# Tokens in another order in SBUF for each pair of feature tiles, in a gated short-convolution layer

## The chip, the core and the metric

The kernel runs on one core of a Trainium2 chip. The metric is the device time of one execution in microseconds; the profile is of one execution on that core. Engines are called as the profile calls them: PE is TensorE, with PEld for its weight loads; DVE is VectorE, ACT is ScalarE, SP the queue that issues nearly all DMAs.

## The reference

One layer, on 256 tokens of 2048 features, in float32. The normalised input is scaled and shifted by a vector that depends on the condition `c`, goes through a large projection to four times 4096 features, a causal convolution of width 3 with gates, and a projection back; then comes a gated residual and a last norm.

```python
h = rmsnorm(x, norm_g[0])
mod = silu(c) @ ada_w[0] + ada_b[0]
shift, scale, gate = split(mod, 3)
h = h * (1 + scale) + shift
b_gate, c_gate, v, g = split(h @ w_in, 4)       # w_in: 2048 x 16384
u = causal_depthwise_conv(c_gate * v, conv_w)   # width 3
y = (b_gate * u * silu(g)) @ w_out              # w_out: 4096 x 2048
out = rmsnorm(x + gate * y, final_g)
```

## The kernel before

**Products in three parts.** Every large product is taken in `float32r`, which keeps fewer bits of the mantissa. To keep float32's accuracy, each operand is split into a high part, rounded to `float32r`, and a low part, the rest. One product becomes three that are added in PSUM: weights high with tokens high, weights high with tokens low, weights low with tokens high.

**The tile of tokens.** `hT` (L272) holds the modulated input, features on the partitions: 16 feature tiles of 128 features, and for each tile a row of 512 words in each partition, the 256 tokens' high parts and behind them the 256 low parts. `hh_` and `hl_` (L273, L274) are views of the two halves. `modulate` (L293) fills it, for two feature tiles at a time: ACT writes the high part (L300), DVE computes the full value in place (L301) and writes the low part (L304).

**The first projection.** The weights are the stationary operand (128 features by 128 outputs), the tokens the moving one (128 features by 256 tokens). `product` (L440) issues one of the three matmuls for a feature tile `k`, at L444. A 128-output tile takes 16 × 3 matmuls of 256 columns, and there are 128 of them, so 6144 in all. PSUM banks hold two such outputs, and only the first matmul into a bank clears its flags (`start`); the other output's first matmul is ordered behind it by hand (L447).

The scale and shift take long to arrive: `ada_w` is read in pieces (`ada_piece`), summed over the rows on DVE, and each group of pieces makes two more feature tiles ready (`ada_done`, `modulate`). Therefore `plan` (L52) writes out by hand, from costs and due times, which part of which output is computed over which feature tiles while the rest is not yet there. `part` (L469) runs such a step (tiles `mm_s`, weights `raw_s`); sums that are not whole are kept in `acc`. That covers the first half of the projection, 16 of 32 column tiles in each quarter. The second half (loop from L573; tiles `mm_b`, weights `raw`) takes all 16 feature tiles at once, in two halves of eight (`KP`). The weights are split by ACT (`split_hi`, L314) and DVE (`split_lo`, L319).

**The gate of the residual** is computed beside this: 32 pieces of `ada_w` (`at_g`, L556) are summed on DVE (L563, L565), and four matmuls of ones (L568) add over the partitions. These instructions are given a lower priority (`later(GIVE)`), and the scheduler places them. It orders the instructions of each engine and queue ahead of time by a model of its own; only what `in_order`, `behind` and `issue_after` mark is fixed by hand.

**The second projection** (`out_mm`, L621) has the tokens as the stationary operand and 512 weight columns as the moving one, three matmuls again (L629 to L631), and ends with the gated residual and the norm.

Of the kernel before, what the change touches and what calls it, by code (L numbers as in the profile page):

```python
# [8 lines left out]
F32 = mybir.dt.float32  # L9
F32R = mybir.dt.float32r  # L10
AF = mybir.ActivationFunctionType
ALU = mybir.AluOpType
# [4 lines left out]
T = 256  # L17
KT = D // P
# [99 lines left out]
def short_conv_layer(ctx: ExitStack, tc: tile.TileContext, x, c, norm_g, ada_w, ada_b, w_in, conv_w, w_out, final_g, out):  # L118
    nc = tc.nc
# [16 lines left out]
    def slot(shape, name, dtype=F32):  # L136
        return slots.tile(shape, dtype, tag="slot", name=name)
# [4 lines left out]
    after = mybir.DependencyInfo(mybir.DependencyClass.NoSync, mybir.DependencyReason.DATA)  # L142
# [104 lines left out]
    bias = vec[:, KT : 3 * KT].rearrange("p (s k) -> p s k", s=2)  # L247
# [6 lines left out]
    for t in range(TT):  # L254
        for dh in range(2):
# [3 lines left out]
            else:  # L259
                nc.vector.scalar_tensor_tensor(  # L260
                    out=junk[:, t], in0=xt[t][dh], scalar=1.0, in1=xt[t][dh], op0=ALU.mult, op1=ALU.mult,
# [8 lines left out]


    hT = hpool.tile([P, KT, 2 * T], F32R, tag="big", name="hT")  # L272
    hh_ = hT[:, :, 0:T]  # L273
    hl_ = hT[:, :, T : 2 * T]  # L274
    xs = [slot([P, CT, T], f"xs{j}") for j in range(KT // CT)]

    def turn_x(j):
# [13 lines left out]
    mod = const.tile([P, 2, KT], F32, tag="mod", name="mod")  # L291

    def modulate(k0, nk, sums):  # L293

        ks = slice(k0, k0 + nk)
        sums = sums.rearrange("p (s k) -> p s k", s=2)
        nc.vector.tensor_tensor(out=mod[:, :, ks], in0=sums, in1=bias[:, :, ks], op=ALU.add)
        for k in range(k0, k0 + nk):
            hf = xs[k // CT][:, k % CT, :]
            nc.scalar.activation(hh_[:, k], hf, AF.Identity, bias=mod[:, 0, k : k + 1], scale=mod[:, 1, k : k + 1])  # L300
            nc.vector.tensor_scalar(  # L301
                out=hf, in0=hf, scalar1=mod[:, 1, k : k + 1], scalar2=mod[:, 0, k : k + 1], op0=ALU.mult, op1=ALU.add
            )
            nc.vector.tensor_tensor(out=hl_[:, k], in0=hf, in1=hh_[:, k].bitcast(F32), op=ALU.subtract)  # L304

    def hi_tile():
        return wpool.tile([P, SLOT], F32R, tag="hi", name="hi", bufs=3)
# [26 lines left out]
    def split(raw, n, lo_tag="lo"):  # L334

        return split_lo(raw, n, split_hi(raw, n), lo_tag)
# [38 lines left out]
    pieces0 = [split(raw0[:, 0 : CT * P], CT * P)]  # L375
    hi0 = [split_hi(raw0[:, k * CT * P : (k + 1) * CT * P], CT * P) for k in range(1, NK0)]
    modulate(0, NK0, sums0.rearrange("p (o f) -> p o f", o=2 * NK0)[:, :, 0])
    tp_3 = turn_x(3)
    pinned.close()
# [49 lines left out]
    def ada_done(k0, nk, gv):  # L429

        tp = psum.tile([P, 4, P], F32, tag="sm", name="tp_g", bufs=2)
        gs = const.tile([P, 4], F32, tag="gs", name="gs", bufs=2)
        for o in range(2 * nk):
            nc.tensor.transpose(tp[:, o, :], gv[:, o // nk, (o % nk) * P : (o % nk + 1) * P], ident)  # L434
        nc.vector.reduce_sum(gs[:, 0 : 2 * nk], tp[:, 0 : 2 * nk, :], axis=mybir.AxisListType.X)
        modulate(k0, nk, gs[:, 0 : 2 * nk])

    opener = [None]

    def product(dst, hi, lo, k, i, begins, left, ends):  # L440

        w, h = ((hi, hh_), (hi, hl_), (lo, hh_))[i]

        mm = last_mm[0] = nc.tensor.matmul(dst, w, h[:, k], start=begins and left, stop=ends, skip_group_check=True)  # L444
        if begins and left:
            opener[0] = mm
        elif begins:  # L447
            tc.add_manual_dep(mm.ins, opener[0].ins.name, after, reason="the bank's flags are cleared first")

    def chunk_products(bank, hi, lo, o0, k, k0, k1, seed=False, late=False):  # L450


        begins = k == k0 and not seed
        terms = [(m, i) for i in (0, 2, 1) for m in range(CT)] if late else [(m, i) for m in range(CT) for i in range(3)]
        for m, i in terms:
            o = slice(o0 + m * P, o0 + (m + 1) * P)
            product(bank[:, m, :], hi[:, o], lo[:, o], k, i, begins and i == 0, m % 2 == 0, k == k1 - 1 and (m, i) == terms[-1])

    last_mm = [None]
# [80 lines left out]
    def gate(dc):  # L540
        return gates[dc // 2][:, dc % 2, :]
# [31 lines left out]
    for ct in range(NS, NCT, 2):  # L573
        for q in QUARTERS:
            bank = psum.tile([P, CT, T], F32, tag="mm", name="mm_b")[:, 0:2]
            col = q * E + ct * P
            for kp in range(0, KT, KP):
                raw = raw_tile("raw")
                nc.sync.dma_start(
                    raw.rearrange("p (k f) -> p k f", k=KP),  # L580
                    w_in[0, kp * P : (kp + KP) * P, col : col + 2 * P].rearrange("(k p) f -> p k f", p=P),
                )
                hi, lo = split(raw, SLOT)
                for m in range(2):
                    for i in range(KP):
                        k = kp + i
                        o = slice((i * 2 + m) * P, (i * 2 + m + 1) * P)
                        for j in range(3):
                            product(bank[:, m, :], hi[:, o], lo[:, o], k, j, k == 0 and j == 0, m == 0, k == KT - 1 and j == 2)
                n_piece += 1  # L590
                if n_piece % 2 == 0:
                    gate_piece()
# [58 lines left out]
    for dc in range(4):  # L651
        dcs = slice(dc * 512, (dc + 1) * 512)

        both = [psum.tile([P, TT, 512], F32, tag="mm", name="mm_o") for _ in range(1 + (dc == 3))]
# [7 lines left out]
        for ep in range(n_ep):  # L662

            first = dc == 0 and ep == 0
# [5 lines left out]
            if dc == 3:  # L670
# [3 lines left out]
                    out=raw3, in0=raw3, in1=gate(dc).unsqueeze(1).to_broadcast([P, EP, 512]), op=ALU.mult  # L674
                )
            hi, lo = split(raw, SLOT, "raw")
# [55 lines left out]
```

## Time and profile before

| | |
|---|---|
| Median of the two runs | 913.5 us (913.44 to 913.55) |
| Span of the profiled execution | 911.9 us |
| Mean granted clock of TensorE | 0.997 |
| PE, PEld, DVE, ACT busy | 98%, 94%, 68%, 51% |
| Before the first product of L444 | 25.3 us |
| First projection (25 to 729 us), L444 | 6144 matmuls, DMA 195 to 356 GB/s by stage |
| Second projection (from 729 us), L629 to L631 | 768 matmuls of 512 columns |

The profiled execution has no time of its own beside its span; the median of the runs is 1.6 us longer than the span, which leaves out what lies around the first and the last instruction. In the profile, a matmul's duration is longer than the distance to the next one, since matmuls follow each other in a pipeline and their ends are modelled: the mean of 276 ns of a group is not what one more matmul costs. That is read from the distance between starts in the timeline. A group's row gives line, engine, operation, tiles, shapes and number, then busy time and the mean of one, then the idle time before them and what ended it.

### The profile page before, as it was taken

What the parts mean: (1) busy time and instruction counts of PE and PEld (TensorE: products, weight loads), DVE (VectorE), ACT (ScalarE), POOL (GpSimd) and SP (SyncE); (2) the same over time, 40 slices, a digit from 0 to 9 for tenths busy, and PEclk for the clock granted to TensorE, in tenths of its full rate; (3) what the DMA queues carried; (4) which work ended last, traced back from release to release, by engine and by line L of the source; (5) the groups of instructions that cost most, each with busy time, mean ns of one, the idle gap of its engine ahead of it and who ended that gap; (6) DMA issues with size and microseconds to landing.
All of it is one profiled execution on the core that took longest, in us unless ns stands there. A gap on an engine that the chain in (4) does not pass through costs nothing.

```text
span 911.9 us, 16239 instructions
## 1 busy us (share of the span) xinstructions
PE 895.7 (98%) x7047; PEld 858.5 (94%) x7047; DVE 616.2 (68%) x593; ACT 464.6 (51%) x413; POOL 0.7 (0%) x6
## 2 busy tenths in 40 slices
PE   6999999999999999999999999999999999999996
PEld 4999999999999999999999999999999988888885
DVE  4889999989888899765545555545554544555882
ACT  6768856665558756743334433444333333443333
POOL 0000000000000000000000000000000000000000
PEclk9999999999999999999999999999999999999998
DMA  9999999999998698676656665566656486655542
GB/s 309 367 371 353 365 325 351 356 369 352 338 328 275 197 359 301 201 246 197 186 188 197 200 201 186 187 195 200 200 188 188 140 331 231 203 201 186 185 139 92
DMA packets 163752, 227.65 MB, mean 250 GB/s; under 512 B 5680, under 2 KB 104160, under 8 KB 163296
## 3 DMA queue, kind: packets, MB, share of 16 engines
q1 hardware_dynamic: 163552, 226.56, 74.8%
q8 instruction: 55, 0.90, 0.4%
q14 instruction: 17, 0.14, 0.0%
q10 hardware_dynamic: 128, 0.04, 0.0%
HBM read 224.49 MB, written 2.10 MB: 248 GB/s over the span
## 4 chain that ended last, share of the span: by engine, by line
PE 94%; DMA 3%; ACT 1%; SPq 1%; DVE 0%; issue 0%; ACTq 0%
PE mm_b L444 38%; PE mm_s L444 36%; PE mm_o L631 6%; PE mm_o L629 6%; PE mm_o L630 6%; DMA raw_s<-in_sc_w_in_dram 2%; DMA at<-in_ada_w_dram 1%; SPq L210 1%; DMA x<-in_x_dram 1%; ACT hi L314 0%; PE ps_gate L568 0%; PE tp_g L434 0%; ACT acc L465 0%; DVE lo L319 0%; ACT hT L300 0%; SPq L413 0%
## 5 line engine op out<-in xcount | busy, mean ns | idle before, releaser
L444 PE MATMUL mm_s<-hT,hi 128*128 128x256 f32 x2048 | 350.5, 277 | 0.2
L444 PE MATMUL mm_b<-hT,hi 128*128 128x256 f32 x2048 | 348.8, 276 | 0.0
L444 PEld LDWEIGHTS mm_s<-hT,hi 128*128 128x128 f32 x2048 | 308.7, 188 | 1.1 <-ACT hT L300 0.4
L444 PEld LDWEIGHTS mm_b<-hT,hi 128*128 128x128 f32 x2048 | 308.7, 188 | 0.2 <-issue 0.2
L444 PE MATMUL mm_b<-hT,lo 128*128 128x256 f32 x1024 | 282.6, 276 | 0.0
L444 PE MATMUL mm_s<-hT,lo 128*128 128x256 f32 x1024 | 282.2, 277 | 0.2 <-DVE lo L319 0.2
L319 DVE TENSOR_TENSOR lo<-raw,hi 128x2048 fp32r<-128x2048 f32 (+1 forms) x66 | 148.0, 2244 | 136.8 <-ACT hi L314 136.8
L314 ACT CAST hi<-raw 128x2048 fp32r<-128x2048 f32 (+1 forms) x66 | 123.7, 1874 | 200.2 <-PE mm_b L444 156.1
L444 PEld LDWEIGHTS mm_b<-hT,lo 128*128 128x128 f32 x1024 | 192.2, 188 | 0.2 <-issue 0.2
L444 PEld LDWEIGHTS mm_s<-hT,lo 128*128 128x128 f32 x1024 | 191.7, 188 | 0.7 <-DVE lo L319 0.6
L319 DVE TENSOR_TENSOR lo<-raw_s,hi 128x2048 fp32r<-128x2048 f32 (+1 forms) x80 | 147.6, 1850 | 25.6 <-ACT hi L314 24.6
L314 ACT CAST hi<-raw_s 128x2048 fp32r<-128x2048 f32 (+1 forms) x80 | 124.2, 1559 | 72.0 <-PE mm_s L444 59.2
L319 DVE TENSOR_TENSOR lo<-raw_o,hi 128x2048 fp32r<-128x2048 f32 x32 | 73.3, 2292 | 66.3 <-ACT hi L314 66.1
L314 ACT CAST hi<-raw_o 128x2048 fp32r<-128x2048 f32 x32 | 61.0, 1907 | 107.2 <-PE mm_o L631 83.7
L630 PE MATMUL mm_o<-lo,y 128*128 128x512 f32 x256 | 99.7, 391 | 0.0
L629 PE MATMUL mm_o<-hi,y 128*128 128x512 f32 x256 | 99.3, 389 | 0.0
L631 PE MATMUL mm_o<-hi,y 128*128 128x512 f32 x256 | 99.3, 389 | 0.0
L427 DVE SCALAR_TENSOR_TENSOR gv<-at,silu_c,gv 128x512 f32<-128x512 f32 x105 | 78.6, 749 | 2.2 <-DMA at<-in_ada_w_dram 0.3
L465 ACT COPY acc<-mm_s 128x1024 f32<-128x1024 f32 x54 | 54.5, 1012 | 35.9 <-PE mm_s L444 35.9
L630 PEld LDWEIGHTS mm_o<-lo,y 128*128 128x128 f32 x256 | 48.1, 188 | 10.2 <-issue 0.2
L631 PEld LDWEIGHTS mm_o<-hi,y 128*128 128x128 f32 x256 | 48.0, 188 | 10.2 <-issue 0.2
L629 PEld LDWEIGHTS mm_o<-hi,y 128*128 128x128 f32 x256 | 48.1, 188 | 9.9
(89 smaller groups left out, 349.6 us busy)
## 6 DMA issues: line engine op xcount, KB each, us to landing
raw<-in_sc_w_in_dram SPq DMA_DIRECT2D x64, 1024.0 KB, 5.7
raw_s<-in_sc_w_in_dram SPq DMA_DIRECT2D x47, 1024.0 KB, 7.9
raw_o<-in_sc_w_out_dram SPq DMA_DIRECT2D x32, 1024.0 KB, 5.1
at<-in_ada_w_dram SPq DMA_DIRECT2D x114, 256.0 KB, 8.0
raw_s<-in_sc_w_in_dram SPq DMA_DIRECT2D x33, 512.0 KB, 7.1
at_g<-in_ada_w_dram SPq DMA_DIRECT2D x32, 512.0 KB, 7.8
at<-in_ada_w_dram SPq DMA_DIRECT2D x6, 512.0 KB, 9.6
x<-in_x_dram SPq DMA_DIRECT2D x4, 512.0 KB, 6.4
```

The costliest lines, as they stand in the source:

```text
L210: nc.sync.dma_start(at[:, :, s, :], adas[:, j : j + kk, s, 0 : NK0 * P])
L314: nc.scalar.copy(hi[:, :n], raw[:, :n])
L319: nc.vector.tensor_tensor(out=lo[:, :n], in0=raw[:, :n], in1=hi[:, :n].bitcast(F32), op=ALU.subtract)
L427: nc.vector.scalar_tensor_tensor(out=gv, in0=at4[:, i], scalar=c_k, in1=gv, op0=ALU.mult, op1=ALU.add)
L444: mm = last_mm[0] = nc.tensor.matmul(dst, w, h[:, k], start=begins and left, stop=ends, skip_group_check=True)
L465: nc.scalar.copy(acc[ch, q], bank)
L629: nc.tensor.matmul(po, yh, hi[:, o], start=opens, stop=False, skip_group_check=True)
L630: nc.tensor.matmul(po, yh, lo[:, o], start=False, stop=False, skip_group_check=True)
L631: nc.tensor.matmul(po, yl, hi[:, o], start=False, stop=ct == NCT - 1, skip_group_check=True)
```

## The change

The row of 512 words that `hT` has for each feature tile is no longer high parts and then low parts for every tile. `tokens(k, low)` gives the view of tile `k`'s high (0) or low (1) parts, and `as_tokens(ap, k)` splits any 256 tokens in the same way, so that writers and readers agree on the order:

| Feature tiles | Where the 256 words of one part lie |
|---|---|
| 0, 1 | in one run, as before |
| 2, 3 | words of the two parts by turns (step of 2 words) |
| 4, 5 | pairs of words by turns |
| 6, 7 | fours by turns |
| 8, 9 | sixteens by turns |
| 10, 11 | in one run, but read in pairs, by turns from its first and its second half |
| 12, 13 | the same in fours |
| 14, 15 | in one run, as before |

Thus the moving operand of a product is read with a step (tiles 2, 3), in runs with gaps (4 to 9), or in runs that jump by 128 words (10 to 13). The order of the tokens in PSUM stays: the output of each matmul is still one run. For tile 15, each product of 256 columns becomes two of 128, with the same weights. The diff:

```diff
     hT = hpool.tile([P, KT, 2 * T], F32R, tag="big", name="hT")
-    hh_ = hT[:, :, 0:T]
-    hl_ = hT[:, :, T : 2 * T]
+
+    def tokens(k, low):
+
+        both = hT[:, k]
+        n = {1: 1, 2: 2, 3: 4, 4: 16}.get(k // 2)
+        if n:
+            return both.rearrange("p (a b n) -> p a b n", b=2, n=n)[:, :, low, :]
+        part = both[:, low * T : (low + 1) * T]
+        n = {5: 2, 6: 4}.get(k // 2)
+        return part.rearrange("p (b a n) -> p a b n", b=2, n=n) if n else part
+
+    def as_tokens(ap, k):
+
+        n = {1: 1, 2: 2, 3: 4, 4: 16}.get(k // 2)
+        if n:
+            return ap.rearrange("p (a n) -> p a n", n=n)
+        n = {5: 2, 6: 4}.get(k // 2)
+        return ap.rearrange("p (a b n) -> p a b n", b=2, n=n) if n else ap
+
...
-            nc.scalar.activation(hh_[:, k], hf, AF.Identity, bias=mod[:, 0, k : k + 1], scale=mod[:, 1, k : k + 1])
+            nc.scalar.activation(
+                tokens(k, 0), as_tokens(hf, k), AF.Identity, bias=mod[:, 0, k : k + 1], scale=mod[:, 1, k : k + 1]
+            )
             nc.vector.tensor_scalar(
                 out=hf, in0=hf, scalar1=mod[:, 1, k : k + 1], scalar2=mod[:, 0, k : k + 1], op0=ALU.mult, op1=ALU.add
             )
-            nc.vector.tensor_tensor(out=hl_[:, k], in0=hf, in1=hh_[:, k].bitcast(F32), op=ALU.subtract)
+            nc.vector.tensor_tensor(
+                out=tokens(k, 1), in0=as_tokens(hf, k), in1=tokens(k, 0).bitcast(F32), op=ALU.subtract
+            )
...
-        w, h = ((hi, hh_), (hi, hl_), (lo, hh_))[i]
-
-        mm = last_mm[0] = nc.tensor.matmul(dst, w, h[:, k], start=begins and left, stop=ends, skip_group_check=True)
-        if begins and left:
-            opener[0] = mm
-        elif begins:
-            tc.add_manual_dep(mm.ins, opener[0].ins.name, after, reason="the bank's flags are cleared first")
+        w, low = ((hi, 0), (hi, 1), (lo, 0))[i]
+        h = tokens(k, low)
+        parts = [slice(0, T)] if k < KT - 1 else [slice(0, T // 2), slice(T // 2, T)]
+        for n, c in enumerate(parts):
+            mm = last_mm[0] = nc.tensor.matmul(
+                as_tokens(dst[:, c], k), w, h if len(parts) == 1 else h[:, c],
+                start=begins and left and n == 0, stop=ends and n == len(parts) - 1, skip_group_check=True,
+            )
+            if begins and left and n == 0:
+                opener[0] = mm
+            elif begins:
+                tc.add_manual_dep(mm.ins, opener[0].ins.name, after, reason="the bank's flags are cleared first")
```

## The prediction

> **What bounds the kernel now.** I read the page's busy rows first, then the chain that ended last, then the groups with shapes kept apart, and at the end the timeline of TensorE, because a pipelined matmul's duration isn't its price.
>
> ```profile
> span 911.9 us, 16239 instructions
> PE 895.7 (98%) x7047; PEld 858.5 (94%) x7047; DVE 616.2 (68%) x593; ACT 464.6 (51%) x413; POOL 0.7 (0%) x6
> ...
> PE   6999999999999999999999999999999999999996
> ...
> DVE  4889999989888899765545555545554544555882
> ACT  6768856665558756743334433444333333443333
> ...
> PEclk9999999999999999999999999999999999999998
> ...
> PE 94%; DMA 3%; ACT 1%; SPq 1%; DVE 0%; issue 0%; ACTq 0%
> PE mm_b L444 38%; PE mm_s L444 36%; PE mm_o L631 6%; PE mm_o L629 6%; PE mm_o L630 6%; DMA raw_s<-in_sc_w_in_dram 2%; DMA at<-in_ada_w_dram 1%; SPq L210 1%; DMA x<-in_x_dram 1%; ACT hi L314 0%; PE ps_gate L568 0%; PE tp_g L434 0%; ACT acc L465 0%; DVE lo L319 0%; ACT hT L300 0%; SPq L413 0%
> ```
>
> TensorE is full from the second slice to the last but one, at the granted full clock, and 74% of the chain is the products of line 444, the line that the change rewrites. VectorE and ScalarE have room everywhere and most of it in the second half. So what a product of line 444 costs more goes into the end, one for one, and what the other two engines do more is hidden.
>
> The groups give the counts, and the timeline the price (columns: start, length, engine, line, tile, shapes, number).
>
> ```profile
> L444 PE MATMUL mm_s<-hT,hi 128*128 128x256 f32 x2048 | 350.5, 277 | 0.2
> L444 PE MATMUL mm_b<-hT,hi 128*128 128x256 f32 x2048 | 348.8, 276 | 0.0
> L444 PE MATMUL mm_b<-hT,lo 128*128 128x256 f32 x1024 | 282.6, 276 | 0.0
> L444 PE MATMUL mm_s<-hT,lo 128*128 128x256 f32 x1024 | 282.2, 277 | 0.2 <-DVE lo L319 0.2
> ```
>
> ```profile
> 720.02 0.28 PE L444 MATMUL mm_b<-hT,lo 128*128 128x256 f32 x1
> 720.14 0.39 PE L444 MATMUL mm_b<-hT,hi 128*128 128x256 f32 x2
> ...
> 729.20 0.28 PE L444 MATMUL mm_b<-hT,lo 128*128 128x256 f32 x1
> 729.32 0.39 PE L629 MATMUL mm_o<-hi,y 128*128 128x512 f32 x1
> ...
> 735.45 0.39 PE L629 MATMUL mm_o<-hi,y 128*128 128x512 f32 x1
> ```
>
> There are 2048 + 2048 + 1024 + 1024 = 6144 products, 384 for each of the 16 feature tiles. From the first to the last `lo` row shown lie 27 rounds of three products in 9.18 us: 113.3 ns a product. The two rows of line 629 are nine rounds of three 512-column products apart, 6.13 us: 227.0 ns. Twice the columns take twice the time, 0.443 ns a column, with nothing left for a fixed part: the stream of the moving operand is the limit, and the weight load before each product (188 ns long in its row below) lies wholly beside it.
>
> **How near the reading is to its limit.** The gate sums are plain fp32 products of 512 contiguous columns, two records each, whose weight loads start one record apart:
>
> ```profile
> 302.25 0.30 PEld L568 LDWEIGHTS ps_gate<-gacc,ones 128*128 128x128 f32 x2
> 302.79 0.19 PEld L568 LDWEIGHTS ps_gate<-gacc,ones 128*128 128x128 f32 x1 [0.24 <-issue]
> 303.22 0.19 PEld L568 LDWEIGHTS ps_gate<-gacc,ones 128*128 128x128 f32 x1 [0.24 <-issue]
> ```
>
> Such a record takes 0.43 us for 512 columns, 0.84 ns a column. The stream of line 444 asks for words at nearly double that rate, and at 0.443 ns it is 5% slower than half of 0.84. I read this as a read path that is at its limit at one word in 0.443 ns, so that words fetched and not used would cost time. It is a reading, not a proof: it tells nothing of the size of a fetch.
>
> **The change, part by part.**
>
> *Stepped and broken runs, tiles 2 to 13.* Number and width of these products stay (12 × 384 = 4608), the PSUM side stays one run of 256 words, and only the moving operand's order differs. No row of this trace has a stepped moving operand. The bounds for one product are 113.3 ns (nothing is lost; a gain would need a stream faster than 0.443 ns a column, for which the only row is the 5% above) and twice that, 226.6 ns, where half of what is fetched is thrown away. By pairs of tiles, 768 products each, the upper end is worth 768 × 113.3 ns = 87.0 us.
> - Words (tiles 2, 3): every second word is skipped, so any fetch wider than one word brings half waste. I take the upper end, +87.0 us, because the path is at its limit in the row above.
> - Pairs (4, 5) and pairs from two halves (10, 11): waste only if a fetch is wider than 8 bytes. Fours (6, 7; 12, 13) and sixteens (8, 9): only if it is wider than 16 or 64 bytes. I take the lower end, 0, for all of these: two columns in one fetch is the least that makes words dear. Both ends stay for the range, most of all for the two pair orders, 2 × 87.0 us.
>
> *Halved products, tile 15.* 384 products of 256 columns become 768 of 128, each with a weight load of its own, so TensorE gets 384 more matmuls and loads. By columns alone a half takes 56.7 ns and the sum is unchanged. But then a load of 128 columns must pass in 56.7 ns too, and the nearest rows with one load for every 128 columns don't show that:
>
> ```profile
> 15.73 1.67 PEld L283 LDWEIGHTS tp_x<-ident,x 128*128 128x128 f32 x15 [0.29 <-issue]
> ...
> 20.02 3.21 PEld L353 LDWEIGHTS sum<-silu_c,at 128*128 128x128 f32 x28
> ```
> ```profile
> L444 PEld LDWEIGHTS mm_s<-hT,hi 128*128 128x128 f32 x2048 | 308.7, 188 | 1.1 <-ACT hT L300 0.4 <-ACT mm_s L477 0.3 <-ACT hi L314 0.2
> L353 PEld LDWEIGHTS sum<-silu_c,at 128*128 128x128 f32 x44 | 5.1, 191 | 0.0
> L283 PEld LDWEIGHTS tp_x<-ident,x 128*128 128x128 f32 x32 | 3.6, 141 | 0.5 <-issue 0.5
> ```
>
> The 15 loads of the transposes span 1.67 us with a last one of 0.141: (1.67 − 0.14) / 14 = 109.3 ns from load to load. The 28 of line 353: (3.21 − 0.19) / 27 = 111.9 ns. No loads stand closer in these streams. Bounds for a half: 56.7 ns (then 0 us), and a half that costs what a 128-column fp32 product costs, two records of 111.9 (line 353 has 22 products and 44 records): 223.8 ns, (447.6 − 113.3) × 384 = 128.4 us. I take the transposes' pace, one load and one record each: (2 × 109.3 − 113.3) × 384 = +40.4 us. These rows could owe their pace to their columns rather than to the load; that is why the lower end stays a rival.
>
> [...]
>
> *Filling hT.* The writes of ScalarE and VectorE into the tile are stepped now, on 12 of 16 tiles:
>
> ```profile
> L300 ACT ACTIVATE hT<-xs,mod x16: 587/594/608, 24.7 to 236.8; 128x256 fp32r<-128x256 f32 x16
> ```
> ```profile
> L304 DVE TENSOR_TENSOR hT<-xs,hT x16: 416/418/426, 25.8 to 241.0; 128x256 fp32r<-128x256 f32 x16
> ```
>
> If each doubled, that were 12 × 0.594 = 7.1 us on ScalarE and 12 × 0.418 = 5.0 us on VectorE. Cover: TensorE works on tiles that are ready meanwhile, and it waits for other engines almost nowhere:
>
> ```profile
> PE tp_v L229 <- DMA rows<-in_ada_b_dram: 4.3, 1, 4.3
> PE tp_v L229 <- DMA rows<-in_c_dram: 4.0, 1, 4.0
> PE mm_s L444 <- DVE lo L319: 0.2, 1, 0.2
> ```
>
> Tiles 0 and 1, which open the stage, keep their order. I take 0; without the cover it is 12 us at most.
>
> *What the scheduler moves.* In the built program 12 of the 32 loads of the gate's weights on SP, with their VectorE sums, no longer stand among the `raw_s` loads but among the `raw` loads, the last of them ahead of 20 remaining `raw` loads. Each `raw` load feeds 48 products, 5.4 us, so over 100 us remain before the output stage, where the gate is read first. SP could hold a `raw` load behind a gate load that waits for its buffer; three `raw` buffers are over 10 us of cover, and VectorE is half idle there (fives in its row). I take 0. If it failed, each such wait would stall TensorE by some us, 12 times at most.
>
> *Sum.* 911.9 (span) + 87.0 + 40.4 = 1039.3 us. The median of the runs shown, 913.5, is 1.6 us over the span: 1041 us.
>
> **The rivals.**
> 1. *Stepping is free at two words or more.* Every order in this change leaves at least two used words in each 16 bytes it passes through. If that is enough, only the halves cost: 911.9 + 40.4 + 1.6 = 954 us. For it: no row shows a penalty; against it: the 5%. [...]
> 2. *A fetch is 16 bytes and TensorE needs all four words.* Then words, pairs and the pairs from two halves double, and fours and sixteens don't: 911.9 + 3 × 87.0 + 40.4 + 1.6 = 1215 us. For it: the same 5%, which would then mean that whole lines just suffice. Against it: nothing here shows the size.
> 3. *Not slower: the second load hides and stepping is free.* If a load passes in 56.7 ns, halves cost nothing, and the time is 913.5, 914 us. For it: the load of line 444 never shows beside 113 ns; against it: both streams above with one load for 128 columns go at 109 to 112 ns. It decides as long as a half takes less than (113.3 + 47.7) / 2 = 80 ns, since 2% of 913.5 is 18.3 us, 47.7 ns on each of 384 products. Were the broken orders to lose the 5% as well, 4608 × some 5 ns = 23 us would come off.
> 4. *Every broken run doubles,* sixteens and fours too: 911.9 + 6 × 87.0 + 40.4 + 1.6 = 1476 us. Nothing speaks for it but that the trace has no such operand.
> 5. *A half runs at the fp32 price,* 128.4 us in place of 40.4: 1129 us with the words' 87.0, 1042 without.
>
> **How the numbers follow.** Forecast 0.27, rival 1 0.24, rival 2 0.25, rival 3 0.07, rival 4 0.07, rival 5 0.10. The likeliest gives 1041 us; its own range, with a half between 100 and 120 ns, is 1030 to 1050. The three large cases are nearly as likely as each other, so the range runs from just under rival 1 to just over rival 2, 948 to 1225 us, and holds 0.86 by the cases, less for mixtures between and beyond them. Within 2% (about what a measurement of this kernel can tell from no change) lies most of rival 3, 0.05; faster is its last sentence, 0.02; slower is all the rest, 0.93.
>
> **What would show it.** In the profile after, the start-to-start of products, tile by tile: 113 ns for tiles 0, 1, 14 and all orders but words, 227 ns for words, 109 ns for each half. Pairs at 227 ns would mean rival 2, words at 113 rival 1, halves at 57 rival 3. TensorE's waits should stay under 10 us; more of them in the second half would mean that the gate's loads hold SP. The forecast is wrong if words run as contiguous columns do, or if an order of two or more words is slower.

## The result, and the profile after

| | before | after |
|---|---|---|
| Median | 913.5 us | 1198.8 us (1198.3 to 1199.2) |
| Span of the profiled execution | 911.9 us | 1196.6 us |
| Mean granted clock of TensorE | 0.997 | 0.999 |

The ratio is 1.312 (95% interval 1.3085 to 1.3162): slower by 285 us, where 127 were forecast. The time lies inside the range and close to rival 2 (1215 us). Page of the profile after, the lines that answer to those of before:

```profile
span 1196.6 us, 16988 instructions
PE 1180.6 (99%) x7431; PEld 1110.2 (93%) x7431; DVE 619.8 (52%) x593; ACT 465.9 (39%) x413; POOL 0.7 (0%) x6
...
PE 99%; DMA 1%; ACT 0%; ACTq 0%; issue 0%; DVE 0%
```

The work of DVE and ACT is what it was (616 and 465 us before), and TensorE is as full as before and 285 us longer. Its waits for other engines are now only the two at the start, so neither the stepped writes into `hT` nor the gate's loads, moved on SP, hold it:

```profile
PE tp_v L229 <- DMA rows<-in_c_dram: 4.3, 1, 4.3
PE tp_v L229 <- DMA rows<-in_ada_b_dram: 3.9, 1, 3.9
```

So the matmuls themselves take longer. The timeline shows a stretch of the second half of the projection in which all 16 tiles come by in order; three products (`hi`, `hi`, `lo`) stand for each tile. Of each pair of tiles the first row is copied:

```profile
600.35 0.39 PE L467 MATMUL mm_b<-hT,hi 128*128 128x256 f32 x2
...
601.04 0.63 PE L467 MATMUL mm_b<-hT,hi 128*128 128x256 f32 x2
...
602.40 0.64 PE L467 MATMUL mm_b<-hT,hi 128*128 128x256 f32 x2
...
603.77 0.43 PE L467 MATMUL mm_b<-hT,hi 128*128 128x256 f32 x2
...
604.50 0.40 PE L467 MATMUL mm_b<-hT,hi 128*128 128x256 f32 x2
...
605.22 0.51 PE L467 MATMUL mm_b<-hT,hi 128*128 128x256 f32 x2
...
606.23 0.43 PE L467 MATMUL mm_b<-hT,hi 128*128 128x256 f32 x2
...
606.99 0.40 PE L467 MATMUL mm_b<-hT,hi 128*128 128x256 f32 x2
...
607.34 0.56 PE L467 MATMUL mm_b<-hT,hi 128*128 128x128 f32 x4
...
607.96 0.45 PE L467 MATMUL mm_b<-hT,hi 128*128 128x256 f32 x2
```

The distance from row to row, divided by six products, is the price: words 1.36 / 6 = 227 ns, pairs 1.37 / 6 = 228, fours 122, sixteens 120, pairs from two halves 168, fours from two halves 127; tile 14 (three products) 117; tile 15 0.62 / 3 = 207, two halves each. The same read over the whole trace, from each matmul's start to the next one's, summed by tiles:

| Tiles, order | before, us | after, us | more, us | forecast, us |
|---|---|---|---|---|
| 0, 1: one run | 88.5 | 91.0 | 2.5 | 0 |
| 2, 3: words by turns | 87.5 | 175.2 | 87.7 | 87.0 |
| 4, 5: pairs by turns | 87.6 | 175.3 | 87.7 | 0 |
| 6, 7: fours by turns | 88.2 | 93.4 | 5.2 | 0 |
| 8, 9: sixteens by turns | 87.4 | 94.4 | 7.0 | 0 |
| 10, 11: pairs from two halves | 87.6 | 129.3 | 41.7 | 0 |
| 12, 13: fours from two halves | 87.2 | 98.0 | 10.8 | 0 |
| 14: one run | 43.6 | 45.1 | 1.5 | 0 |
| 15: halved products | 43.6 | 82.9 | 39.3 | 40.4 |

The rows add up to 283 us, against 284.7 between the spans: almost nothing is left for another cause. What asks for one is why pairs cost as much as words, why pairs from two halves cost half of that, and what a half waits for.

### The profile page after: what moved, and what is told of

Same layout as the page of the kernel before. It is cut to its first block, busy times and chain, and to the rows that moved or that the text cites. A ratio compares the mean times of both kernels' runs of the same rounds, so it can differ in the third digit from the quotient of the medians.

```text
span 1196.6 us, 16988 instructions
## 1 busy us (share of the span) xinstructions
PE 1180.6 (99%) x7431; PEld 1110.2 (93%) x7431; DVE 619.8 (52%) x593; ACT 465.9 (39%) x413; POOL 0.7 (0%) x6
## 4 chain that ended last, share of the span: by engine, by line
PE 99%; DMA 1%; ACT 0%; ACTq 0%; issue 0%; DVE 0%
PE mm_b L467 41%; PE mm_s L467 41%; PE mm_o L655 5%; PE mm_o L656 5%; PE mm_o L657 5%; PE tp_idle L237 1%; DMA rows<-in_ada_b_dram 1%; PE sum L374 0%; PE ps_gate L594 0%; PE tp_g L455 0%; PE tp_x L300 0%; ACT big L674 0%; ACT big L716 0%; ACTq L754 0%; ACT hT L317 0%
## 5 line engine op out<-in xcount | busy, mean ns | idle before, releaser
L467 PE MATMUL mm_b<-hT,hi 128*128 128x256 f32 (+1 forms) x2176 | 478.7, 321 | 0.0
L467 PE MATMUL mm_s<-hT,hi 128*128 128x256 f32 (+1 forms) x2176 | 477.0, 321 | 0.1
L467 PEld LDWEIGHTS mm_b<-hT,hi 128*128 128x128 f32 x2176 | 365.0, 195 | 12.6 <-issue 1.4
L467 PEld LDWEIGHTS mm_s<-hT,hi 128*128 128x128 f32 x2176 | 363.8, 194 | 10.6 <-ACT hT L317 0.3
L467 PE MATMUL mm_s<-hT,lo 128*128 128x256 f32 (+1 forms) x1088 | 338.5, 322 | 0.0
L467 PE MATMUL mm_b<-hT,lo 128*128 128x256 f32 (+1 forms) x1088 | 337.6, 320 | 0.0
L467 PEld LDWEIGHTS mm_b<-hT,lo 128*128 128x128 f32 x1088 | 206.9, 195 | 5.7
L467 PEld LDWEIGHTS mm_s<-hT,lo 128*128 128x128 f32 x1088 | 206.0, 194 | 6.0 <-DVE lo L340 0.2
L335 ACT CAST hi<-raw_o 128x2048 fp32r<-128x2048 f32 x32 | 61.0, 1907 | 113.3 <-PE mm_o L657 86.2
```

Source lines behind the costliest of these rows:

```text
L335: nc.scalar.copy(hi[:, :n], raw[:, :n])
L467: mm = last_mm[0] = nc.tensor.matmul(as_tokens(dst[:, c], k), w, h if len(parts) == 1 else h[:, c], start=begins and left and n == 0, stop ...
```

## The experiments

All kernels keep the two functions of the change, `tokens` and `as_tokens`, with a table of orders by pair of tiles and a table of cuts. The theory to begin with (**L**): the stream of the moving operand pays for each aligned line of 16 bytes that it enters 1.77 ns, an estimate from one run (113.3 ns / 64 lines), however many of the line's four words are used. Its rival (**S**): what counts is how many consecutive words a run has. For the halves, **W**: a weight load of 128 columns takes about 108 ns (82.9 us / 768 halves in tile 15) and isn't hidden by 56.7 ns of stream; **M** and **A** are stated below.

**Halves alone.** No other order; tile 15 still halved.

```diff
+    ORDERS = {}
+    SPLITS = {15: (128,)}
```

> All tiles in one run as before; only tile 15's products are halved. If the halves cost what the profile after shows (a start every 108 ns or so, 216 ns for a product in place of 113): 384 x 103 ns = 39 us, 953 us. If part of the 285 us comes from the halves in another way (flags, order of work, what follows them), the time is above 965; if a half costs only its columns, 914.

Measured: 958.7 us, ratio 1.0493 (1.0475 to 1.051): 6 us more than the 953 expected. Tile 15 takes 39.1 us more, as expected; another 4 us are in tiles 0 and 8 of the second half, which come right behind the halves half of the time; they take 124.6 ns on the mean there. So the halves cost 45 us in all, and in the changed kernel tile 15 takes the same: the halves add up with the rest.

**Undo words and pairs.** Tiles 2 to 5 are put into fours by turns; everything else stays, and they are still stepped.

```diff
-        n = {1: 1, 2: 2, 3: 4, 4: 16}.get(k // 2)
+        n = {1: 4, 2: 4, 3: 4, 4: 16}.get(k // 2)
```

> The changed kernel with words and pairs by turns (tiles 2 to 5) put into fours by turns as tiles 6 and 7 are; all else as changed, still stepped. If the unit is 16 bytes these four tiles cost 119 ns a product in place of 228: 4 x 384 x 109 ns = 167 us less than 1199, 1031 us. If stepped tiles cost by their number (any stepped operand), no change: 1199.

Measured: 1028.6 us, ratio to the kernel before 1.1258 (1.1241 to 1.1274). The four tiles take 118 to 119 ns a product. Fours by turns cost 5% over the 113.3 ns of one run; words and pairs by turns, which use half of each aligned 16 bytes, cost 100% (227 and 228 ns).

**Six orders, no halves.** Lines or runs, and what far places do.

```diff
+    ORDERS = {1: ('inside', 0), 2: ('across', 0), 3: ('quarters', 2), 4: ('turns', 8), 5: ('far', 2), 6: ('halves', 1)}
...
+    SPLITS = {}
...
+        if kind == "far":
+            return both.rearrange("p (b s a n) -> p s a b n", b=2, s=2, n=n)[:, low]
...
+        if kind == "inside":
+            return part.rearrange("p (a b c) -> p a c b", b=2, c=2)
+        if kind == "across":
+            four = both.rearrange("p (a x n) -> p a x n", x=4, n=2)
+            return four[:, :, 0:4:3, :] if low else four[:, :, 1:3, :]
```

`far` reads from two places 1 KB apart by turns, `inside` reads words 0, 2, 1, 3 of each line, and `across` puts the high parts into words 2 to 5 of every eight and the low parts into words 0, 1, 6, 7.

> No halves. Six orders, read tile by tile from the distance of the starts. Theory L (the stream pays 1.77 ns for each aligned 16-byte line that it enters, whatever it uses of it; order inside a line is free): tiles 2, 3 (words 0, 2, 1, 3 of each line) 113 ns; tiles 4, 5 (fours that lie across two lines, and pairs from two lines) 227 for high and low; tiles 8, 9 (eights by turns) 113 to 121. Theory S (what counts is the length of a run of consecutive words, wherever it lies; short runs are dear): tiles 2, 3 227; tiles 4, 5 119 for the high parts, whose runs are four long, and 227 for the low; eights 113 to 121. For both open: tiles 6, 7 (pairs from four quarters by turns) between 167 and 227; tiles 10, 11 (pairs from two places 1 KB apart) 167 as at 512 bytes if distance does not matter; tiles 12, 13 (words from two halves by turns) 334 if each entry costs 1.3 ns as in the pairs from halves, 453 if 1.77. Whole: L 1258 to 1395 us, S 1290 to 1430.

The kernel was run once; its timeline, again the first row of each pair of tiles. The first block has tiles 2, 4 and 6 and the row after tile 7, the second tiles 8, 10, 12 and 14:

```profile
650.42 0.39 PE L497 MATMUL mm_b<-hT,hi 128*128 128x256 f32 x2
...
651.10 0.63 PE L497 MATMUL mm_b<-hT,hi 128*128 128x256 f32 x2
...
652.46 0.66 PE L497 MATMUL mm_b<-hT,hi 128*128 128x256 f32 x2
...
653.82 0.43 PE L497 MATMUL mm_b<-hT,hi 128*128 128x256 f32 x2
```
```profile
657.98 0.43 PE L497 MATMUL mm_b<-hT,hi 128*128 128x256 f32 x2
...
658.72 0.50 PE L497 MATMUL mm_b<-hT,hi 128*128 128x256 f32 x2
...
659.72 0.39 PE L497 MATMUL mm_b<-hT,hi 128*128 128x256 f32 x2
...
660.39 0.40 PE L497 MATMUL mm_b<-hT,hi 128*128 128x256 f32 x2
```

Words 0, 2, 1, 3 of a line: 0.68 / 6 = 113 ns, though no two neighbours in it are read in turn. Fours across two lines: 1.36 / 6 = 227 on the mean, where S has 155 (two of three products at 119), though the high runs are as long as in tiles 6 and 7 of the change. Both go against S and with L. Eights take 123 here, 119 over the run (the median, as in all such figures below). Pairs from four quarters take 227 (225 over the run), pairs from 1 KB apart 167, as from 512 bytes. But words from two halves take 0.67 / 6 = 112 ns, where every form of L had 334 or more; the whole is 1139 us, below both theories' sums. L as stated falls: with one word from each line in turn it should be slowest, and it is faster than one run.

This makes a new theory, **P**, an estimate fitted to these prices; what inside TensorE makes them, no run shows. It counts the even and the odd columns of a product apart, side by side. A word counts 0.84 ns, the time of a column in the fp32 records of the kernel before (0.43 us for 512 columns). In each count the present line and the one before are at hand: a return to that one costs nothing beside the word. A line that isn't at hand comes 1.77 ns (the time of a line in one run) after the count's last new line at the earliest. Words from two halves give each count a half of its own: four words from a line, 3.4 ns, no loss, 107.5 ns a product. Pairs from two halves make each count go A, B, A, B between two lines: two new lines, 3.54 ns, and two returns, 1.68 ns, for eight columns: 167 ns in all, as measured. One run gives two words from each line, 1.77 ns in place of 1.68, which is the 113.3 ns.

**More orders.** P was fitted to the run above; this one tests it. L1 is one count for all columns, with the same two lines at hand and half of P's 0.84 ns for a word.

```diff
+    ORDERS = {1: ('steps', 4), 2: ('quarters', 1), 3: ('two lines', 4), 4: ('far', 4), 5: ('halves', 16), 6: ('steps', 8)}
...
+        if kind == "steps":
+            return part.rearrange("p (a w) -> p w a", w=n)
+        if kind == "two lines":
+            return part.rearrange("p (a l w) -> p a w l", l=2, w=n)
```

> Tile by tile. [...] Tiles 2, 3 (step of four words, a new line for each column): P 227 ns, L1 453. Tiles 4, 5 (words from four quarters by turns): P 137, L1 453. Tiles 6, 7 (words by turns from two lines that lie side by side): P 112 (the load's pace), L1 193, and if only far lines can be held together 227 or more. Tiles 8, 9 (fours from two places 1 KB apart): 126 as fours from halves. Tiles 10, 11 (sixteens from halves): 113 to 121. Tiles 12, 13 (step of eight words): as the step of four, unless the distance of lines counts.

The kernel was run once and took 1126 us. The rows are the first of tiles 2, 4 and 6 and the row after tile 7:

```profile
641.91 0.63 PE L505 MATMUL mm_b<-hT,hi 128*128 128x256 f32 x2
...
643.29 0.46 PE L505 MATMUL mm_b<-hT,hi 128*128 128x256 f32 x2
...
644.14 0.39 PE L505 MATMUL mm_b<-hT,hi 128*128 128x256 f32 x2
...
644.81 0.40 PE L505 MATMUL mm_b<-hT,hi 128*128 128x256 f32 x2
```

Step of four words: 1.38 / 6 = 230 ns (233 over the run), where L1 has 453. Words from four quarters: 0.85 / 6 = 142, against 137 and 453. Words from two neighbouring lines: 0.67 / 6 = 112, against 193. Over the run, fours from 1 KB apart take 127 ns, sixteens from halves 120, the step of eight 219. In the three orders that part the theories P holds to some 4%, and L1 is out. What P leaves open: the step of eight is 6% faster than that of four, and full lines that don't follow each other (fours, eights, sixteens, fours from halves) take 119 to 127 ns where P has 113.

**Cuts.** What a half waits for. Tile 11 has loads of 64 weight columns (the second half of its outputs is left out, and added to the first).

```diff
+    SPLITS = {11: (128,), 12: (192,), 13: (224,), 14: (64, 128, 192), 15: (128,)}
...
+        rows = [(slice(0, P), c) for c in parts] if k != 11 else [(r, c) for c in parts for r in (slice(0, 64), slice(64, P))]
...
+                as_tokens(dst[0 : r.stop - r.start, c], k), w[:, r], h if len(parts) == 1 else h[:, c],
```

> All tiles in one run. Tile 15 cut 128+128, tile 14 into four of 64, tile 13 224+32, tile 12 192+64; tile 11 cut 128+128 with weights of 64 columns, two loads for each (the second half of its outputs is left out, and added to the first). Theory W (a load of 128 weight columns takes some 108 ns and nothing but the load before it delays it; 64 columns take half): tile 15 216 ns a product, tile 14 432, tiles 13 and 12 216 each, tile 11 four times 57 = 227. Theory M (every matmul takes 108 ns at least, whatever its load): the same but tile 11 432. Theory A (each matmul costs its columns and 52 ns more, when it is cut): tile 14 322, tile 11 322, the others 216. Whole: W about 1200 us, M about 1280.

The kernel was run once. The rows are the first of tiles 11 to 15, with the `lo` row of tile 11:

```profile
961.90 0.64 PE L498 MATMUL mm_b<-hT,hi 128*64 128x128 f32 x8
962.38 0.40 PE L498 MATMUL mm_b<-hT,lo 128*64 128x128 f32 x4
962.62 0.58 PE L498 MATMUL mm_b<-hT,hi 128*128 128x192 f32 x4
...
963.26 0.60 PE L498 MATMUL mm_b<-hT,hi 128*128 128x224 f32 x4
...
963.93 1.06 PE L498 MATMUL mm_b<-hT,hi 128*128 128x64 f32 x8
...
965.27 0.64 PE L498 MATMUL mm_b<-hT,hi 128*128 128x128 f32 x4
```

Tile 11: twelve matmuls in 0.72 us, 60 ns each, 240 ns a product: W's 227, not M's 432 or A's 322. Tile 12: 0.64 / 3 = 213 ns; tile 13: 223; tile 14, twelve matmuls: 1.34 / 3 = 447, 112 ns each with only 64 columns of stream. So a matmul with 128 weight columns follows the one before by some 112 ns, although its stream is only 64 columns long. With half the weight columns 128 columns of stream pass in 60 ns, hardly more than the 56.7 that half of 113.3 makes, so the floor there is 60 ns at most. It goes with the number of weight columns; that it is the load itself, and not something else that goes with them, these runs don't show. Below, the floor is called the load's for short. The theories can be compared only where the granted clock is full, as in this stretch (1.00 from 955 to 971 us). The whole came to 1346 us, over both sums; in part of it the granted clock was lower, 0.71 on the mean from 250 to 600 us (last section).

**One step on: even and odd columns each in a half of their own.** Words from two halves cost 112 ns, which by P and W is the load's floor and not the stream's. So all 16 tiles in that order, no cuts; then also the second projection, whose 512-column products (227.0 ns before) leave the load's 112 ns room.

```diff
+    ORDERS = {j: ("halves", 1) for j in range(8)}
+    SPLITS = {}
```

> All 16 tiles read as tiles 12, 13 of the six orders, which took 112 ns: words from the two halves of the part by turns; no halved products. If those 112 ns hold for all: 6144 x 1.6 ns = 10 us less than before, 904 us. If the 112 came from what stood beside those tiles, 913. Theory W adds that it can't go under the 112 ns of a weight load.

Measured: 904.3 us, ratio 0.9894 (0.9881 to 0.9908). Nearly all products take 111.7 ns; these two rows are ten rounds of three apart, 3.35 us:

```profile
716.06 0.39 PE L497 MATMUL mm_b<-hT,hi 128*128 128x256 f32 x2
...
719.41 0.39 PE L497 MATMUL mm_b<-hT,hi 128*128 128x256 f32 x2
```

Then the second projection as well:

```diff
-            nc.tensor.matmul(po, yh, hi[:, o], start=opens, stop=False, skip_group_check=True)
+            nc.tensor.matmul(by_turns(po), yh, from_halves(hi[:, o]), start=opens, stop=False, skip_group_check=True)
```

(The other two products alike; the write that seeds `po` and the two reads that need its order go through the same views.)

> As the one before, and the second projection's 512 weight columns are read in the same order (the outputs lie permuted in PSUM, and its readers put them back). [...] If the gain of the order is always the same 1.4%, 224 ns and 902; if the order gains nothing and only the load's pace was seen, 904.

```profile
724.78 0.38 PE L692 MATMUL mm_o<-hi,y 128*128 128x512 f32 x1
...
727.37 0.38 PE L692 MATMUL mm_o<-hi,y 128*128 128x512 f32 x1
```

Four rounds of three products in 2.59 us: 215.8 ns for 512 columns, against 227.0 before; 256 words at P's 0.84 ns make 215. Measured: 895.0 us, ratio to the kernel before 0.9799 (0.9786 to 0.9813): faster than both kernels, under the kernel before by about 2%, and under the 902 us of an equal gain of 1.4%.

## Why the prediction was wrong

- **Where the time goes, and that nothing hides it**: right. 283 of the 285 us are distances between the starts of the products that line 444 issued; TensorE waits for nothing new, so the moved gate loads cost nothing that shows. The writes into `hT` need no cover: ScalarE's median went from 594 to 601 ns, VectorE's from 418 to 420.
- **Words, +87.0 us**: the number is right, 87.7, the price behind it is not. It was worked out as half of the fetch thrown away; but the step of four words throws away three quarters and costs 230 ns, no more than the step of two. By P's count, the even and the odd columns each enter a new line at every word in both: 128 × 1.77 = 227 ns.
- **Pairs by turns, taken at the lower end, 0**: this step failed, and is the largest error: 87.7 us. The prediction put it as "two columns in one fetch is the least that makes words dear" and chose that least; no row showed the size. The prices go by aligned 16-byte lines: fours that lie across two lines cost 227 ns, four words of one line 113, in both orders tried. By P's count, pairs by turns give the even and the odd columns one word each in a line.
- **Pairs from two halves, 0**: failed by the same step, 41.7 us. By P's count they cost less than pairs by turns because a return to the line before counts 0.84 ns and not 1.77; P was fitted to the 167 ns, and in its test the three orders that part it from L1 came out within 4%. P remains an estimate that fits the prices; no run shows what makes them.
- **Fours, sixteens, fours from halves, 0**: 5.2 + 7.0 + 10.8 = 23.0 us. That they are far cheaper than half-used lines is right, that they are free is not; why lines that aren't in sequence take 6 to 12% more here stays open. The unchanged tiles 0, 1 and 14 add 4.0 us; with the halves alone, such an extra stood in the tiles right behind them.
- **Halves, +40.4 us**: right, 39.3 in tile 15 (45 us for the kernel with halves alone), and the pace that goes with the weight columns is what was forecast: 112 ns behind full loads with 64 columns of stream, 60 ns at most behind half loads. Part of it is luck. The 109.3 ns came from transposes of fp32 data, and 128 columns at the 0.84 ns of the fp32 records make 107.5 ns too: whether those rows showed their loads or their columns, no run settles. The pace of the weights, which the prediction saw lie wholly beside the stream, was less than 2 ns from being the limit itself: 111.7 against 113.3.
- **The 5%** by which full-rate reading was slower than half of an fp32 record's pace (0.443 ns a column against 0.42) was read as a read path at its limit, and unused words did cost time: 227 ns for words by turns. In words from two halves the 5% is gone: 512 columns take 215.8 ns, half of a record's 0.43 us is 215. It spoke for rival 2 as much as for the forecast: if the unit is a line of four words, one run uses all four and already loses 5%, so a line with two used words could not keep up. The rows did not decide between the two; the prediction stopped at the smallest unit that the words needed.
- **Rivals.** Rival 2 was right for words and pairs by turns, wrong for pairs from halves (41.7 in place of 87.0), and without the 27 us of small terms; 1215 against 1199. Rival 1 (two used words in 16 bytes suffice) fell with the pairs at 227 ns. Both orders with two used words of a line in turn, words and pairs, cost the same, 87.7 us each. Counted by P, those are one word for the even and one for the odd columns, where one run has two for each. Rivals 3 (halves free), 4 (sixteens dear) and 5 (halves at 224 ns) fell: a half takes 108 ns and a product in sixteens 120 to 123.
- **Together.** The time came out 158 us over the forecast, and the two pair orders are 129 us of that.

## What to carry to other kernels

Where the stream of the moving operand bounds TensorE, as here, ask of each order how often the even and the odd columns change 16-byte lines, not how long the runs are: by turns in words or pairs doubled the price (227 and 228 ns against 113.3), whole lines that don't follow each other cost 5 to 12% (119 to 127 ns). Giving even and odd columns a place of their own took 2% off a kernel that was full of contiguous products (895.0 us, ratio 0.9799). A product must stream long enough to cover the pace of its weights; with 128 columns of float32r weights that was 112 ns, and cutting a 256-column product in two nearly doubled its time (82.9 us for 384 products, 216 ns against 113.3).

## What was not expected of the hardware

A contiguous float32r stream wasn't the fastest: 512 columns take 227.0 ns, where words by turns from two halves take 215.8. An order that jumps 1 KB at every word was cheaper here than one without a jump.

In the kernel with the cuts the granted clock was lower in part of the run, with TensorE busy throughout. In the rows stand the stretch and its length, the busy time of PE, PEld, DVE, ACT and POOL, then the mean clock, the DMA share and GB/s:

```profile
100.00:250.00 150.00, 150.00 (x1434) 150.00 (x1433) 130.40 (x148) 87.12 (x73) 0.00 (x0) 1.00 1.02 341
250.00:600.00 350.00, 350.00 (x2510) 350.00 (x2510) 90.93 (x94) 85.69 (x81) 0.00 (x0) 0.71 0.27 87
...
700.00:1100.00 400.00, 400.00 (x3774) 398.57 (x3774) 164.56 (x135) 111.26 (x82) 0.00 (x0) 1.00 0.47 148
```

In that stretch the matmuls of tile 14 stand 111 ns apart from 509.84 to 510.73 us, and from 511.18 us on 204 to 214 ns:

```profile
511.18 1.82 PE L498 MATMUL mm_s<-hT,hi 128*128 128x64 f32 x8
512.81 1.04 PE L498 MATMUL mm_s<-hT,lo 128*128 128x64 f32 x4
513.66 1.90 PE L498 MATMUL mm_s<-hT,hi 128*128 128x64 f32 x8
```

Twelve matmuls of 64 columns in 2.48 us are 207 ns each. The mean granted clock was 0.80 from 504 to 516 us, where this change falls, and 1.00 from 955 to 971 us, where they take 112 ns. So the slower pace came where the granted clock was lower. Why the clock fell is not shown; with halves alone, one cut tile in place of five, it was 1.00 from 100 to 600 us. Whether the number of cuts is the reason was not tried further.
